# A diagonal state-space branch whose scratch transfers are issued by GpSimd instead of SyncE

## The chip, the cores and the metric

The kernel runs on one core of one Trainium2 chip. The metric is the device time of one execution in microseconds (us). Before the change it is 2403.66 us, the median of three executions that lie between 2402.31 and 2406.75 us.

## What is computed

The reference is a trunk of two layers over 272 positions (16 learned ones and 256 of the input) of width 2048, in float32. An even layer projects the normalised input to queries, keys, values and a 512 wide signal u. The first three feed grouped-query attention (12 heads, 4 key heads, rotary positions), u feeds a bidirectional diagonal complex state-space model (S5) in 32 groups of 16 channels with 64 states each; both are concatenated and projected back. An odd layer does the same with retention and an mLSTM. Each layer ends with a squared-ReLU MLP of width 8192. Only the S5 branch of the even layer matters here. Cut to its core:

```python
def s5_direction(u, lam_re, lam_im, log_dt, b_re, b_im, c_re, c_im):
    ...
    bu_re = jnp.einsum('blgh,gph->blgp', u, bbar_re)
    bu_im = jnp.einsum('blgh,gph->blgp', u, bbar_im)
    ...
    _, _, x_re, x_im = lax.associative_scan(_complex_scan_combine, (a_re, a_im, bu_re, bu_im), axis=1)
    return jnp.einsum('blgp,ghp->blgh', x_re, c_re) - jnp.einsum('blgp,ghp->blgh', x_im, c_im)
```

## The kernel before

**Weights.** Every projection is one `stream` (lines 144 to 206). It loads a stripe of the weights, 128x1024 float32 or 512 KB, into a tile `raw` (line 184, issued by SyncE; line 181 where a stripe is put together from two parts). ScalarE rounds it to `wh` (line 134), VectorE takes the rest, `wl` (line 135), and TensorE adds three products per block, wh by xh, wh by xl and wl by xh (line 168). `raw`, `wh` and `wl` have four buffers each, so a load of `raw` waits until `wl` of the stripe four before it is made.

**The even layer.** `even_in` first streams the weights of u (`w_u`, eight stripes). `first_norm` then finds the norm of the input, and for each of the four blocks of u `evac_u` scales the block into `up` (line 741) and stores it to a DRAM scratch `s5_u` (line 744). `finish_u` gathers it back as `U` with time folded by eight: eight transfers, one for each residue s, each of 16 partitions by 32 groups by 34 steps (line 751), so that its contiguous runs are 34 floats, 136 bytes. Behind that the stripes of q, k and v follow (`w_even`, 40 stripes of 512 KB) with the attention.

**The S5 branch** is a generator that is woven into that stream. It goes through eight batches of four groups. `batch` loads the coefficients `bc` (line 835, 256 KB, two buffers), scales them (line 837), builds on VectorE the tables `W` and `CA` (helper `tt`, line 754), transposes W to `WT` on TensorE (line 876), and multiplies `kps` (line 887). `CA` goes to a DRAM scratch `s5_ca` (line 890, 576 KB, one buffer for CA) for use at the end. Out of `kps` come the taps `Kf`, and eight shifted copies of `Kf` make the stripes of `M` (line 900, eight transfers of 32 KB a batch). `apply` multiplies `U` by `WT` into `pe` (line 913) and by `M` into `pm` (line 922). After the last batch the recurrence over the 34 folded steps runs on VectorE; `tail` loads `CA` again (line 979), multiplies, applies GELU and the half-GLU, and the output projection follows.

**Who sets the order.** Each engine, and each engine's issue of transfers, takes its instructions strictly in order, and an instruction that waits holds up all behind it on that engine. The order is not that of the program text. A planner makes it when the program is built, out of priorities (`high_priority` in `stream`, `batch`, `run`) and of its own model of what each instruction occupies: a transfer counts as work of the engine that issues it. SyncE (SP in the profile) issues nearly all transfers: weights, hT, u, U, bc, CA, M. GpSimd (POOL) issues four loads of constants at the start (lines 101, 545, 546, 548), and in the even layer it otherwise runs some memsets (`pt2` L578, `qr` and `sq` L598, `V` L661, the first column of EE L947); the adds of the residuals (L307) come after the layer. All of this is queued by

```python
nc.sync.dma_start(out=self.ud[ft * P:(ft + 1) * P], in_=up)
nc.sync.dma_start(out=self.U[s * 16:(s + 1) * 16], in_=v[s])
nc.sync.dma_start(out=bc, in_=I["s5_bc"][:, b])
nc.sync.dma_start(out=self.cad[b], in_=CA.rearrange("p d g t h -> p (d g t h)"))
```

Of the kernel before, what the change touches and what calls it, by code (L numbers as in the profile page):

```python
# [15 lines left out]
P = 128  # L16
# [707 lines left out]
class S5:  # L724
# [12 lines left out]
    def evac_u(self, ft):  # L737
        nc = self.nc
        acc = self.T.h[:, ft]
        up = self.p2.tile([P, S5C, S5J], F32, name="up", tag="sg")  # L740
        nc.vector.tensor_tensor(out=up.rearrange("p s j -> p j s"),
                                in0=acc.rearrange("p (j s) -> p j s", s=S5C),
                                in1=self.T.rb.rearrange("p (j s) -> p j s", s=S5C), op=ALU.mult)
        nc.sync.dma_start(out=self.ud[ft * P:(ft + 1) * P], in_=up)

    def finish_u(self):
        nc = self.nc
        self.U = self.p1.tile([P, S5G, S5J], F32, name="U")
        v = self.ud.rearrange("(g h) s j -> s h g j", h=16)
        for s in range(S5C):  # L750
            nc.sync.dma_start(out=self.U[s * 16:(s + 1) * 16], in_=v[s])

    def tt(self, out, a, b, op):
        self.nc.vector.tensor_tensor(out=out, in0=a, in1=b, op=op)
# [75 lines left out]
    def batch(self, b):  # L830
        nc, I, p1, p2, tt, T = self.nc, self.I, self.p1, self.p2, self.tt, self.T
        mul, add, sub = ALU.mult, ALU.add, ALU.subtract
        g0 = b * NB
        bc = p2.tile([P, 4, 2, NB, 16], F32, name="bc")
        nc.sync.dma_start(out=bc, in_=I["s5_bc"][:, b])
        bb = p1.tile([P, 2, 2, NB, 16], F32, name="bb")
        nc.vector.tensor_scalar_mul(out=bc[:, 2:], in0=bc[:, 2:], scalar1=self.sg[:, 1:2])
        btmp = p1.tile([P, 2, NB, 16], F32, name="btmp")

        def gsel(x):  # L840
            return x.rearrange("p (d g) -> p d g", d=2)[:, :, g0:g0 + NB].unsqueeze(3).broadcast_to([P, 2, NB, 16])

        cr, ci = gsel(self.cr), gsel(self.ci)
        tt(bb[:, 0], bc[:, 0], cr, mul)
        tt(btmp, bc[:, 1], ci, mul)
        tt(bb[:, 0], bb[:, 0], btmp, add)
        tt(bb[:, 1], bc[:, 1], cr, mul)
        tt(btmp, bc[:, 0], ci, mul)
        tt(bb[:, 1], bb[:, 1], btmp, sub)
        yield  # L850

        def table(dst, tmp, Pa, Pb, A, B, d, lo, n, rev):
            ks = slice(lo, lo + n)

            def pw(x):
                v = x[:, ks, d * S5G + g0:d * S5G + g0 + NB]
                if rev:
                    v = v[:, ::-1]
                return v.rearrange("p k g -> p g k").unsqueeze(3).broadcast_to([P, NB, n, 16])

            def cf(x):
                return x.unsqueeze(2).broadcast_to([P, NB, n, 16])

            tt(dst, pw(Pa), cf(A), mul)
            tt(tmp, pw(Pb), cf(B), mul)
            tt(dst, dst, tmp, add)

        W = p1.tile([P, 2, NB, S5C, 16], F32, name="W")
        wt = p1.tile([P, NB, 9, 16], F32, name="wtmp")
        WT = p1.tile([P, 2, NB, P], F32, name="WT")  # L870
        for d in range(2):
            table(W[:, d], wt[:, :, :S5C], self.P1, self.P2, bb[:, 0, d], bb[:, 1, d], d, 0, S5C, d == 0)
            with T.tc.high_priority(offset=URGENT):
                pt = T.mx([P, NB, P], "wtp")
                for g in range(NB):
                    nc.tensor.transpose(pt[:, g], W[:, d, g].rearrange("p s h -> p (s h)"), T.ident)
                nc.scalar.copy(out=WT[:, d], in_=pt)
            yield
        CA = p1.tile([P, 2, NB, 9, 16], F32, name="CA")
        kp = []  # L880
        for d in range(2):
            table(CA[:, d], wt, self.P1, self.P2, bc[:, 2, d], bc[:, 3, d], d, 0, 9, d == 1)
            with T.tc.high_priority(offset=URGENT):
                ps = T.mx([16, NB, P], "kps")
                for g in range(NB):
                    lo = 0 if d == 0 else 1
                    nc.tensor.matmul(ps[:, g], bb[:, 0, d, g], CA[:, d, g, lo:lo + 8], start=True, stop=True)  # L887
            kp.append(ps.rearrange("p g (t h) -> p g t h", h=16))
            yield
        nc.sync.dma_start(out=self.cad[b], in_=CA.rearrange("p d g t h -> p (d g t h)"))  # L890
        Kf = p1.tile([16, NB, 15, 16], F32, name="Kf")
        nc.scalar.copy(out=Kf[:, :, 8:15], in_=kp[0][:, :, 1:8])
        nc.scalar.copy(out=Kf[:, :, 0:8], in_=kp[1])
        tt(Kf[:, :, 7], kp[0][:, :, 0], Kf[:, :, 7], add)
        dm = p1.tile([16, NB, 16], F32, name="dm")
        tt(dm, self.drow[:, g0:g0 + NB], T.ident[:16, :16].unsqueeze(1).broadcast_to([16, NB, 16]), mul)
        tt(Kf[:, :, 7], Kf[:, :, 7], dm, add)
        M = p1.tile([P, NB, P], F32, name="M")
        for s in range(S5C):
            nc.sync.dma_start(out=M[s * 16:(s + 1) * 16].rearrange("p g (t h) -> p g t h", h=16),  # L900
                                in_=Kf[:, :, 7 - s:15 - s])
        yield
        self.batches.append((b, WT, M))
# [533 lines left out]
```

## Time and profile before

| | |
|---|---|
| median of three executions | 2403.66 us |
| the profiled execution, its own time | 2401.9 us |
| its span, first to last instruction | 2400.1 us |
| TensorE busy | 2347.3 us, 98% of the span |
| VectorE, ScalarE, GpSimd busy | 60%, 47%, 3% |
| mean granted TensorE clock | 0.991 |
| transfers | 415.52 MB, 173 GB/s over the span |

Times in the trace are us from the first instruction. The span is 1.8 us shorter than the time of its execution. A line of the waits reads: who waited, for whom, us in total, how often, the longest. In a timeline a bracket holds the idle time of the engine ahead of the instruction and what ended it. SPq and POOLq are the queues from which SyncE and GpSimd issue transfers; an issue's own duration is the time that the queue was held, and the transfer lands later.

### The profile page before, as it was taken

To read this page: it belongs to the slowest core of one execution; us is meant where nothing else is said; L and a number is where in the kernel's file an instruction comes from. 1 tells how busy PE (TensorE), PEld (TensorE's weight loads), DVE (VectorE), ACT (ScalarE), POOL (GpSimd) and SP (SyncE) were. 2 spreads that over 40 slices of the span, in tenths; PEclk is the share of its full clock that TensorE was granted. 3 is DMA by queue.
4 is the path that set the end of the run, shared out by engine and by line. 5 is a ranking of instruction groups with operands and counts; after the bars stand their busy time and mean duration, and the time that the engine had idled before them with its cause. 6 is when DMAs were issued, how large, how long until landed. Compare 5 with 4: busy or idle time off the path is not lost.

```text
span 2400.1 us, 42631 instructions
## 1 busy us (share of the span) xinstructions
PE 2347.3 (98%) x17287; PEld 2241.3 (93%) x17287; DVE 1442.0 (60%) x2365; ACT 1136.9 (47%) x1768; POOL 60.3 (3%) x116
## 2 busy tenths in 40 slices
PE   7999999999999999999989999999999999999998
PEld 7889899999999999999989999999988988988987
DVE  8786837754554454555679767656744545555555
ACT  6566735543443343344466434444544443443443
POOL 0000001100000000000110000001000000000000
PEclk9999999999999999999999999999999999999999
DMA  8545364555555555555443443564655556555554
GB/s 267 167 148 175 116 200 139 185 175 175 174 177 174 176 175 176 175 176 183 149 150 127 159 150 129 188 198 137 201 186 187 186 173 191 185 186 191 185 187 147
DMA packets 143461, 415.52 MB, mean 173 GB/s; under 512 B 24496, under 2 KB 41280, under 8 KB 142496
## 3 DMA queue, kind: packets, MB, share of 16 engines
q1 hardware_dynamic: 142816, 412.36, 53.9%
q8 instruction: 135, 2.21, 0.4%
q14 instruction: 62, 0.51, 0.1%
q0 software_dynamic: 160, 0.35, 0.1%
q10 hardware_dynamic: 288, 0.10, 0.0%
HBM read 401.62 MB, written 7.95 MB: 171 GB/s over the span
## 4 chain that ended last, share of the span: by engine, by line
PE 90%; DVE 5%; ACT 2%; issue 1%; DMA 1%; POOL 0%; SPq 0%; DVEq 0%; ACTq 0%; POOLq 0%
PE acc L168 82%; DVE wl L135 1%; ACT wh L134 1%; PE kps L887 1%; PE pe L913 1%; PE mo L1221 1%; PE po L710 1%; PE ro L1297 1%; POOL h L307 0%; PE sc L687 0%; DVE res L304 0%; DMA raw<-in_w_u 0%; PE ptp L703 0%; PE ms L1183 0%; PE rs L1288 0%
## 5 line engine op out<-in xcount | busy, mean ns | idle before, releaser
L135 DVE TENSOR_TENSOR wl<-raw,wh 128x1024 fp32r<-128x1024 f32 (+2 forms) x744 | 888.3, 1195 | 808.4 <-ACT wh L134 806.4
L134 ACT CAST wh<-raw 128x1024 fp32r<-128x1024 f32 (+2 forms) x744 | 759.9, 1023 | 1011.8 <-PE acc L168 977.1
L168 PE MATMUL acc<-xh,wh 128*128 128x272 f32 (+1 forms) x3728 | 1070.2, 288 | 18.0 <-ACT wh L134 8.7
L168 PE MATMUL acc<-xh,wl 128*128 128x272 f32 (+1 forms) x3728 | 1070.9, 288 | 11.2 <-DVE wl L135 11.1
L168 PE MATMUL acc<-xl,wh 128*128 128x272 f32 (+1 forms) x3728 | 1070.8, 288 | 3.4 <-DVE xl L135 2.3
L168 PEld LDWEIGHTS acc<-xh,wh 128*128 128x128 f32 x3728 | 706.2, 190 | 21.6 <-ACT wh L134 9.0
L168 PEld LDWEIGHTS acc<-xh,wl 128*128 128x128 f32 x3728 | 707.1, 190 | 15.9 <-DVE wl L135 14.4
L168 PEld LDWEIGHTS acc<-xl,wh 128*128 128x128 f32 x3728 | 708.7, 190 | 5.4 <-DVE xl L135 2.5
L168 PE MATMUL acc<-h1l,wh 128*128 128x272 f32 x1024 | 295.4, 288 | 0.0
L168 PE MATMUL acc<-h1h,wl 128*128 128x272 f32 x1024 | 295.2, 288 | 0.0
L168 PE MATMUL acc<-h1h,wh 128*128 128x272 f32 x1024 | 294.0, 287 | 0.0
L168 PE MATMUL acc<-wh,h1l 128*128 128x512 f32 (+1 forms) x528 | 205.1, 388 | 0.0
L168 PE MATMUL acc<-wh,h1h 128*128 128x512 f32 (+1 forms) x528 | 204.8, 388 | 0.0
L168 PE MATMUL acc<-wl,h1h 128*128 128x512 f32 (+1 forms) x528 | 203.9, 386 | 0.0
L168 PEld LDWEIGHTS acc<-h1h,wh 128*128 128x128 f32 x1024 | 192.9, 188 | 0.0
L168 PEld LDWEIGHTS acc<-h1l,wh 128*128 128x128 f32 x1024 | 192.6, 188 | 0.0
L168 PEld LDWEIGHTS acc<-h1h,wl 128*128 128x128 f32 x1024 | 192.4, 188 | 0.0
L168 PEld LDWEIGHTS acc<-wh,h1l 128*128 128x128 f32 x528 | 99.1, 188 | 22.0
L168 PEld LDWEIGHTS acc<-wl,h1h 128*128 128x128 f32 x528 | 99.3, 188 | 21.7
L168 PEld LDWEIGHTS acc<-wh,h1h 128*128 128x128 f32 x528 | 99.4, 188 | 21.1
L307 POOL TENSOR_TENSOR h<-h,res 128x272 f32<-128x272 f32 (+1 forms) x42 | 43.8, 1053 | 568.0 <-DVE res L304 568.0
L382 ACT ACTIVATE relu<-acc 128x272 f32<-128x272 f32 (+1 forms) x128 | 48.7, 387 | 17.6 <-PE acc L168 17.6
(319 smaller groups left out, 1506.5 us busy)
## 6 DMA issues: line engine op xcount, KB each, us to landing
raw<-in_w SPq DMA_DIRECT2D x480, 512.0 KB, 3.5
raw<-in_w_odd SPq DMA_DIRECT2D x88, 512.0 KB, 3.4
raw<-in_w_even SPq DMA_DIRECT2D x40, 512.0 KB, 4.4
raw<-in_wo_odd SPq DMA_DIRECT2D x24, 512.0 KB, 3.6
raw<-in_wo_a SPq DMA_DIRECT2D x24, 384.0 KB, 4.3
raw<-in_w SPq DMA_DIRECT2D x32, 256.0 KB, 2.6
s_ca<-CA SPq DMA_DIRECT2D x8, 576.0 KB, 3.3
CA<-s_ca SPq DMA_DIRECT2D x8, 576.0 KB, 4.3
```

The source lines that it names most:

```text
L134: nc.scalar.copy(out=hi, in_=src)
L135: nc.vector.tensor_tensor(out=lo, in0=src, in1=hi.bitcast(F32), op=ALU.subtract)
L168: nc.tensor.matmul(a, lt, rt, start=k == 0 and j == 0, stop=k == nk - 1 and j == 2)
L307: eng.tensor_tensor(out=self.h[:, k, t0:], in0=self.h[:, k, t0:], in1=t[:, :N], op=ALU.add)
L382: nc.scalar.activation(out=t[:, :N], in_=acc, func=AF.Relu)
L710: nc.tensor.matmul(po[:, :R // 2], cur["v", g][:, j], PT[j][:, c0:c0 + R // 2], start=j == 0, stop=j == 2)
L887: nc.tensor.matmul(ps[:, g], bb[:, 0, d, g], CA[:, d, g, lo:lo + 8], start=True, stop=True)
L913: nc.tensor.matmul(pev[:, d, g], WT[:, d, g], U[:, g0 + g], start=True, stop=True)
L1221: nc.tensor.matmul(po[:, d, :HD + 1], e[:, t:t + P], V[:, st], start=j == 0, stop=j == len(keys) - 1)
L1297: nc.tensor.matmul(po[:, :HD], w[:, j, t:t + P], self.rvt[:, h, j], start=j == 0, stop=j == 2)
```

## The change

The four stores of `up`, the eight gathers of `U`, the eight loads of `bc` and the eight stores of `CA` (28 transfers) are issued by GpSimd. The 64 stripes of `M`, all weights, and all of the tail stay on SyncE.

```diff
@@ evac_u @@
-        nc.sync.dma_start(out=self.ud[ft * P:(ft + 1) * P], in_=up)
+        nc.gpsimd.dma_start(out=self.ud[ft * P:(ft + 1) * P], in_=up)
@@ finish_u @@
-            nc.sync.dma_start(out=self.U[s * 16:(s + 1) * 16], in_=v[s])
+            nc.gpsimd.dma_start(out=self.U[s * 16:(s + 1) * 16], in_=v[s])
@@ batch @@
-        nc.sync.dma_start(out=bc, in_=I["s5_bc"][:, b])
+        nc.gpsimd.dma_start(out=bc, in_=I["s5_bc"][:, b])
@@ batch @@
-        nc.sync.dma_start(out=self.cad[b], in_=CA.rearrange("p d g t h -> p (d g t h)"))
+        nc.gpsimd.dma_start(out=self.cad[b], in_=CA.rearrange("p d g t h -> p (d g t h)"))
```

## Rows read from the trace of the kernel before

**Rows 1.** The page: busy time, share of the span and instructions by engine.

```profile
PE 2347.3 (98%) x17287; PEld 2241.3 (93%) x17287; DVE 1442.0 (60%) x2365; ACT 1136.9 (47%) x1768; POOL 60.3 (3%) x116
```

**Rows 2.** Busy time by stretch: us, engines (instructions), granted clock, DMA share, GB/s.

```profile
54.90:73.00 18.10, 15.51 (x112) 15.29 (x112) 11.83 (x19) 3.87 (x7) 0.00 (x0) 0.91 0.67 127
73.00:126.00 53.00, 51.79 (x406) 47.31 (x406) 40.80 (x94) 33.54 (x67) 0.17 (x1) 1.00 0.52 171
126.00:202.00 76.00, 75.43 (x552) 67.11 (x552) 56.33 (x126) 53.82 (x111) 0.71 (x4) 1.00 0.47 149
202.00:232.00 30.00, 30.00 (x241) 28.66 (x240) 21.34 (x34) 15.56 (x28) 0.21 (x1) 1.00 0.60 171
```

**Rows 3.** Waits of SyncE's queue over the whole span.

```profile
SPq L900 <- DVE Kf L754: 27.1, 8, 6.2
...
SPq L890 <- DVE CA L754: 14.2, 6, 7.9
...
SPq L835 <- DVE dm L754: 6.0, 1, 6.0
```

**Rows 4.** SyncE's queue in order of time, 41 to 70 us (equal neighbours are merged).

```profile
41.70 6.27 SPq L900 DMA_DIRECT2D M<-Kf  x8
48.07 1.01 SPq L744 DMA_DIRECT2D s_u<-up  x2
...
49.62 0.45 SPq L184 DMA_DIRECT2D raw<-in_w_even  x1
51.40 0.86 SPq L744 DMA_DIRECT2D s_u<-up  x2
52.35 0.89 SPq L184 DMA_DIRECT2D raw<-in_w_even  x2
54.91 6.41 SPq L751 DMA_DIRECT2D U<-s_u  x8
69.27 0.34 SPq L890 DMA_DIRECT2D s_ca<-CA  x1
69.73 0.35 SPq L184 DMA_DIRECT2D raw<-in_w_even  x1
```

**Rows 5.** Waits of TensorE from 40 to 70 us, then from 70 to 100 us.

```profile
PE acc L168 <- DVE wl L135: 2.6, 1, 2.6
...
PE acc L168 <- DVE wl L135: 0.6, 1, 0.6
```

**Rows 6.** ScalarE, then VectorE, in order of time, 44 to 76 us.

```profile
53.98 1.05 ACT L134 CAST wh<-raw 128x1024 fp32r<-128x1024 f32 x1 [7.39 <-DMA raw<-in_w_even]
58.06 0.40 ACT L624 ACTIVATE sqt<-acc 128x272 f32<-128x272 f32 x1 [3.03 <-PE acc L168]
...
59.85 2.00 ACT L134 CAST wh<-raw 128x1024 fp32r<-128x1024 f32 x2
...
75.71 0.35 DVE L837 TENSOR_SCALAR bc<-bc,sgn 128x256 f32<-128x256 f32 x1 [6.46 <-DMA bc<-in_s_bc]
```

**Rows 7.** Moved issues (ns min/median/max, first, last start); one issue of GpSimd (timeline).

```profile
L751 SPq DMA_DIRECT2D U<-s_u x8: 340/488/2629, 54.9 to 60.7; - x8
...
L835 SPq DMA_DIRECT2D bc<-in_s_bc x8: 328/435/897, 5.1 to 159.5; - x8
...
L890 SPq DMA_DIRECT2D s_ca<-CA x8: 326/326/338, 36.6 to 213.6; - x8
...
1.94 0.54 POOL L545 DMA_DIRECT2D cosE<-in_rope_even  x1
```

**Rows 8.** Who needs U first, and median us from issue to landing.

```profile
L913 PEld LDWEIGHTS pe<-U,WT x128: 186/192/192, 72.6 to 221.6; 128*128 128x128 f32 x128
...
s_u<-up SPq DMA_DIRECT2D x4, 136.0 KB, 2.9
U<-s_u SPq DMA_DIRECT2D x8, 68.0 KB, 5.7
...
cosE<-in_rope_even POOLq DMA_DIRECT2D x1, 136.0 KB, 5.7
```

## The prediction

> **What bounds the kernel now.** The first view is the page's busy time: TensorE is busy for 98% of the span and GpSimd for 3% [rows 1]. A change of issuing queues can therefore win only what TensorE loses in the stage where the moved transfers run, so the second view is the stretches of that stage. In the last of them, 202 to 232 us, TensorE runs 241 instructions in 30 us, 8.03 per us [rows 2]; I take this as its full rate. At that rate the 18.1 us from 54.9 would hold 145 instructions and hold 112: 33 are missing, 4.1 us. From 73 to 126 us 426 would fit and 406 are there: 2.5 us. From 126 to 202 us 610 would fit and 552 are there: 7.2 us [rows 2]. There the attention's softmax runs, with VectorE and ScalarE busy for 56 and 54 of 76 us.
>
> The third view is what SyncE's queue waits for. It waits 14.2 us ahead of the stores of CA and 6.0 us once ahead of a load of bc; all that time the weights queued behind are not issued. It also waits 27.1 us ahead of the stripes of M [rows 3], and those stay. The timeline of that queue shows the place: after the first eight stripes of M it issues two stores of u, a load of raw, two stores more, two loads of raw, then eight gathers of U in 6.41 us, and it stands until 69.27 us at a store of CA with the next raw behind it [rows 4]. The fourth view asks whether late weights are what TensorE waits for. Its recorded waits there are 2.6 us for wl in the first 30 us, and 0.6 us for wl later [rows 5]. ScalarE has waited 7.39 us for raw before the cast at 53.98 us, but the next cast, at 59.85 us, stands behind evacuations that start at 58.06 us, once TensorE's accumulation is over [rows 6]: late weights make themselves felt here through the order of ScalarE's queue.
>
> **The change part by part.**
>
> *SyncE's queue.* It loses 28 issues: four of u in 1.87 us [rows 4], eight of U by 0.488, eight of bc by 0.435 and eight of CA by 0.326 us [rows 7], together 1.9 + 3.9 + 3.5 + 2.6 = 11.9 us of issuing, and the 14.2 us and 6.0 us of waits. By itself that is worth nothing: the engine computes nothing, and TensorE covers it with stripes already loaded.
>
> *The weights behind it.* The three loads of raw at 49.62, 52.35 and 52.8 us could leave from 47.97 us on, where the stripes of M end [rows 4], as their buffers come free: up to 1.6, 4.4 and 4.8 us earlier. The raw at 69.73 us could leave up to 7 us sooner, for no issue is left ahead of it. How much reaches TensorE depends on the order in which the planner then puts casts and evacuations. If the order on the other engines stays, nothing does: TensorE has enough to do up to 58 us, and the evacuations still stand ahead of the second cast. If the earlier stripe lets the cast go ahead of them, the wait of 2.6 us is gone. The ends are 0 and the 6.6 us that the two stretches lose (4.1 + 2.5). I take the waits that the profile records, 2.6 + 0.6 = 3.2 us: ScalarE sits idle before the first cast for longer than a cast takes, and the planner charges a transfer to the engine that issues it, so in its model too the weights get earlier.
>
> *bc.* VectorE idles 6.46 us at 75.71 us for bc [rows 6], whose load was queued behind the gathers and a store of CA. It has two buffers, so on GpSimd's queue it can leave when its buffer is free, if nothing there waits ahead of it. Gain: nothing beyond the 3.2 us, since TensorE is busy while VectorE idles.
>
> *u and U.* The last store of u is issued at about 51.9 us, lands 2.9 us later [rows 8], and the first gather follows at 54.91 us [rows 4]: it waits for a landing, not for SyncE. Here GpSimd can lose. One of its issues held its queue for 0.54 us [rows 7], but that transfer had 128 runs and a gather has 16 x 32 = 512. The lower bound is 0.34 us, the shortest on SyncE; the upper 4 x 0.54 = 2.2 us, runs in proportion. I take 1.0 us, nearer to 0.54, the only price of this queue: eight gathers are out by 62.9 us and, with 5.7 us to land [rows 8], U is there at 68.6 us. TensorE first reads it at 72.6 us [rows 8]. Cost 0, with 4 us to spare; the point from which it costs is 1.5 us a gather (54.9 + 8 x 1.5 + 5.7 = 72.6).
>
> *CA.* A store leaves when the table is ready, as now (the one at 69.27 us stood at the head of its queue). The next batch's table needs the single buffer back; the eight stores lie between 36.6 and 213.6 us [rows 7], 25 us apart in the mean, which covers a landing even at the 5.7 us of GpSimd's transfer [rows 8]. Cost 0.
>
> *GpSimd's queue.* 28 issues by 0.54 us are 15.1 us, or by the upper bound for U 28 us, on an engine that runs five instructions between 73 and 202 us [rows 2]. They are memsets of the attention, and some wait for TensorE; a bc behind one, or a memset behind a store of CA, inherits its wait. VectorE waits for bc, ScalarE's copy of V for the memset. I cost this at nothing: the waits of one engine's order are exchanged for those of another with far fewer members.
>
> *Sum.* 2401.9 us, the profiled execution (span 2400.1 and 1.8 around it), less 3.2 is 2398.7. That execution lies 1.8 us under the median, 2403.7, so against the median the forecast is 2403.7 - 3.2 = **2400.5 us**, 0.13% less. About 0.2% of it, 4.8 us, is what a measurement of this kernel can tell from no change.
>
> **The rivals.**
>
> *A, hidden anyway.* The stripes of M stay with their 27.1 us of waits, so weights are still queued behind waiting transfers, and no cast moves ahead of an evacuation. For it: only 3.2 us of TensorE's waits are recorded at all. Against it: the one idle stretch of ScalarE is ended by raw itself. Time 2403.7 us. The Trainium skill, page "DMA: Bandwidth & Descriptors", section "Issuing engines are not separate DMA queues", gives this result by a rule: transfers run on the same 16 engines whoever issues them, and several issuers save only the time of issuing, usually small. By that rule the time stays 2403.7 us; the trace agrees as far as the issues alone go (11.9 us, off the path), but the queue's in-order waits, 14.2 us for CA alone, are moved too.
>
> *B, the whole loss comes back.* With weights, bc and tables earlier, TensorE runs at full rate from 54.9 to 126 us: 6.6 us, 2397.1 us. For it: half of the queue's waits go, and VectorE's idle 6.46 us lies right before the stretch where it is busiest. Against it: the evacuations and the tables stay in order. If the better order also fills the attention's stretch, 7.2 us more, 2389.9 us.
>
> *C, U comes late.* GpSimd makes the 512 runs of each gather at the upper price: the last is out at 54.9 + 8 x 2.2 = 72.5 us, landed at 78.2 us, and pe, which was to start at 72.6 us, holds TensorE's queue for 5.6 us with all products behind it. Time 2409.3 us, slower. For it: the only priced transfer of that queue has a quarter of the runs. Against it: the planner can put other products ahead of pe. It decides the sign above 1.5 us a gather and passes 0.2% above 2.1 us. If the stores of u also land in 5.7 instead of 2.9 us, 2.8 us more, 2412.1 us.
>
> **How the numbers follow.** The forecast has 0.36, with a range of its own of 2398 to 2403: its terms may come out between half and one and a half, and of its chance 0.08 lies beyond 4.8 us of gain. A has 0.13, B 0.28, C 0.23, of which 0.01 stays within 4.8 us. So faster 0.28 + 0.08 = 0.36, within 0.2% 0.28 + 0.13 + 0.01 = 0.42, slower 0.22. The range is 2390 to 2411 us: from B with its attention stretch to C short of its late stores. It leaves out some 0.1 on each side, where the planner's new order moves work that no row here ties to the moved transfers.
>
> **What would show it.** Right: SyncE's queue shows raw right behind the first eight stripes of M; its waits ahead of CA and bc are gone and those of M still there; TensorE's wait of 2.6 us near 58 us is gone; from 54.9 to 126 us some 25 instructions more; the gathers of U on GpSimd's queue 1 us apart, landed before pe. Wrong: TensorE waiting for U at pe; a cast still behind the evacuations, with the same rates (A); or a difference that arises after 232 us, where none of the moved transfers runs, which would mean that the planner's order, not the queue's waits, sets the result.

## The result, and the profile after

The changed kernel takes 2417.35 us, the median of four executions between 2415.65 and 2418.65 us; the kernel before, run beside it, takes 2403.02 us. The ratio on record is 1.0051, with a 95% interval from 1.0039 to 1.0063: 0.51% or some 12 us slower, where 0.13% faster was forecast. (It is not the quotient of the two medians, which is 1.0060 and lies inside the interval.) The two executions that were profiled lie further apart than the medians, 14.3 us: their spans are 2416.8 and 2400.1 us, so what follows accounts for 16.7 us.

The page of the changed kernel, its first part, answers to [rows 1].

```profile
PE 2354.2 (97%) x17287; PEld 2244.7 (93%) x17287; DVE 1443.4 (60%) x2365; ACT 1137.2 (47%) x1768; POOL 76.0 (3%) x144
```

GpSimd has 28 instructions more, the transfers. TensorE does the same work and is busy for 6.9 us more (its mean granted clock is 0.987 against 0.991), so of the 16.7 us at least 9.8 are spent standing. Where, is read from the stretches. First the changed kernel:

```profile
28.00:41.70 13.70, 10.87 (x81) 9.34 (x80) 13.70 (x22) 9.95 (x12) 1.08 (x2) 1.00 0.82 298
41.70:54.90 13.20, 12.86 (x94) 12.33 (x93) 10.36 (x26) 7.30 (x12) 1.30 (x3) 0.93 0.71 231
54.90:73.00 18.10, 18.10 (x139) 17.92 (x139) 15.29 (x24) 5.96 (x8) 7.20 (x12) 0.96 0.72 152
73.00:126.00 53.00, 53.00 (x429) 50.90 (x429) 39.45 (x70) 29.07 (x49) 1.62 (x3) 1.00 0.57 187
126.00:202.00 76.00, 75.25 (x568) 68.36 (x567) 55.38 (x130) 49.32 (x101) 3.94 (x10) 1.00 0.44 145
202.00:232.00 30.00, 27.39 (x177) 22.84 (x175) 20.19 (x41) 19.86 (x45) 0.90 (x3) 0.94 0.17 49
232.00:299.00 67.00, 63.38 (x436) 55.75 (x437) 47.46 (x172) 48.56 (x109) 0.16 (x1) 0.95 0.50 161
299.00:347.00 48.00, 47.63 (x349) 45.40 (x348) 23.59 (x68) 17.22 (x30) 0.00 (x0) 0.93 0.56 170
347.00:400.00 53.00, 47.94 (x334) 45.48 (x334) 28.43 (x46) 21.71 (x37) 0.00 (x0) 0.94 0.60 176
```

Then the stretches of the kernel before that do not stand in [rows 2]:

```profile
28.00:41.70 13.70, 12.33 (x92) 11.03 (x93) 13.70 (x26) 9.53 (x12) 0.00 (x0) 1.00 0.77 266
41.70:54.90 13.20, 13.20 (x103) 12.72 (x103) 9.09 (x23) 5.29 (x9) 0.21 (x1) 1.00 0.54 166
232.00:299.00 67.00, 64.13 (x434) 56.89 (x433) 56.98 (x214) 49.22 (x110) 0.17 (x1) 0.97 0.45 142
299.00:347.00 48.00, 47.79 (x342) 46.34 (x342) 15.21 (x27) 15.82 (x26) 0.00 (x0) 0.93 0.70 204
347.00:400.00 53.00, 52.17 (x418) 51.95 (x416) 34.65 (x56) 26.44 (x43) 0.00 (x0) 1.00 0.55 169
```

Count TensorE's instructions against before. From 28 to 54.9 us there are 20 fewer (175 against 195). From 54.9 to 202 us, where the forecast expected a gain, there are 66 more (1136 against 1070): that gain came, and larger than forecast. Then 64 fewer from 202 to 232 us, 9 more up to 347 us, and 84 fewer from 347 to 400 us. The balance from 28 us on is 93 fewer at 400 us, which at 8.03 per us is 11.6 us. The gain is early, the loss late.

The chain of waits of both kernels, up to 440 us, says what is late. Before:

```profile
72.93 1.71 PE pe L913 x16
...
335.00 4.25 DMA gT<-s_y
339.38 7.57 PE glu L1005 x32
346.95 49.86 PE acc L168 x399
402.43 0.85 PE pb L243 x6
```

After:

```profile
52.49 36.88 PE acc L168 x279
89.37 1.71 PE pe L913 x16
...
355.09 4.00 DMA gT<-s_y
359.22 9.75 PE glu L1005 x32
368.97 43.88 PE acc L168 x351
...
416.18 1.48 PE pb L243 x6
```

The changed kernel's wait of TensorE for a cast, between 300 and 370 us, which the kernel before does not have:

```profile
PE acc L168 <- ACT wh L134: 4.1, 1, 4.1
```

The first product of U into pe is at 89.4 instead of 72.9 us, 16.4 us later. In the chain the next batches' pe follow at 98.5, 113.6 and 129.8 us where before they stood at 83.1, 97.7 and 115.1: some 15 us late, and the last at 238.4 against 220.2, 18 us late. The half-GLU behind the tail starts 19.8 us late. Behind it TensorE has 351 products of the stream left instead of 399, since 48 more are done already; at 49.86/399 = 0.125 us each that gives 6.0 us back. The GLU itself takes 9.75 instead of 7.57 us, 2.2 us more: TensorE has run out of cast weights ahead of it, waits 4.1 us until 357.2 us, and the granted clock during the GLU is 0.77, before 1.00. From the last of these products to pb it takes 2.3 us less. So pb, the broadcast of the norm with which the even layer's output is closed, comes 19.8 + 2.2 - 6.0 - 2.3 = 13.7 us later (416.18 - 402.43 = 13.75). From there to the end the two take about the same, 2000.6 and 1997.7 us; these 2.9 us are the rest of the 16.7.

And pe is not held up by U. TensorE's recorded waits from 55 to 75 us are gone altogether, and no wait of pe for U is among those up to 130 us. What stands ahead of pe is other work, 52.49 to 89.37 us without a gap in the chain. One of the three products of a block, counted up to the first pe, first before, then after:

```profile
L168 PE MATMUL acc<-xh,wh x120: 283/288/592, 8.5 to 72.4; 128*128 128x272 f32 x120
```

```profile
L168 PE MATMUL acc<-xh,wh x164: 282/288/596, 7.1 to 88.8; 128*128 128x272 f32 x164
```

Three products each: 360 of the stream ahead of the first pe before, 492 after. The planner has put 132 products more in front of it.

The moved transfers themselves, in the timelines of SyncE's and of GpSimd's queue after, answer to [rows 4]:

```profile
42.88 5.73 SPq L900 DMA_DIRECT2D M<-Kf  x8
48.71 42.95 SPq L184 DMA_DIRECT2D raw<-in_w_even  x16
...
50.99 0.55 POOL L744 DMA_DIRECT2D s_u<-up  x1 [11.40 <-DVE up L741]
59.39 0.54 POOL L744 DMA_DIRECT2D s_u<-up  x1 [0.37 <-DVE up L741]
62.03 5.00 POOL L751 DMA_DIRECT2D U<-s_u  x8 [2.10 <-DMA s_u<-up]
```

The groups by tile (issues and landings) and the wait of SyncE for M, after, answer to [rows 3, 7, 8]:

```profile
L751 POOL DMA_DIRECT2D U<-s_u x8: 628/628/652, 62.0 to 66.4; - x8
DMA to landing us min/median/max: 6.2/8.4/9.0
...
L835 POOL DMA_DIRECT2D bc<-in_s_bc x8: 536/538/561, 4.3 to 174.4; - x8
...
L890 POOL DMA_DIRECT2D s_ca<-CA x8: 531/542/570, 39.1 to 230.5; - x8
...
SPq L900 <- DVE Kf L754: 44.7, 6, 24.5
```

raw follows the first eight stripes of M at once, SyncE's waits for CA and bc are gone, a gather holds GpSimd's queue for 0.628 us. But u is scaled later (up from 50.1 to 58.4 us; before 46.9 to 51.2), the gathers leave at 62.0 instead of 54.9 us and land in 8.4 instead of 5.7 us, and SyncE once waits 24.5 us ahead of a stripe of M, with weights behind it: the transfers of 202 to 232 us fall from 171 to 49 GB/s.

### The profile page after: what moved, and what is told of

Its sections match the earlier page's. It is cut to its first block, busy times and chain, and to the rows that moved or that the text cites. A ratio compares the mean times of both kernels' runs of the same rounds, so it can differ in the third digit from the quotient of the medians.

```text
span 2416.8 us, 42664 instructions
## 1 busy us (share of the span) xinstructions
PE 2354.2 (97%) x17287; PEld 2244.7 (93%) x17287; DVE 1443.4 (60%) x2365; ACT 1137.2 (47%) x1768; POOL 76.0 (3%) x144
## 4 chain that ended last, share of the span: by engine, by line
PE 87%; DVE 5%; ACT 3%; DMA 2%; issue 1%; POOL 1%; SPq 0%; DVEq 0%; ACTq 0%; POOLq 0%
PE acc L168 79%; DVE wl L135 2%; ACT wh L134 1%; DVE res L304 1%; POOL h L307 1%; PE pe L913 1%; PE kps L887 1%; PE mo L1221 1%; ACT pe L692 1%; PE po L710 0%; PE ro L1297 0%; DVE z L754 0%; PE glu L1005 0%; PE pc L233 0%; DVE xl L138 0%
## 5 line engine op out<-in xcount | busy, mean ns | idle before, releaser
L168 PEld LDWEIGHTS acc<-xh,wh 128*128 128x128 f32 x3728 | 706.5, 190 | 26.5 <-ACT wh L134 12.0
```

The lines of the kernel that those rows point to most:

```text
L168: nc.tensor.matmul(a, lt, rt, start=k == 0 and j == 0, stop=k == nk - 1 and j == 2)
```

## The experiments

Three theories. **P**, the planner's order: with U's gathers on GpSimd it puts some 130 products ahead of the first pe, and the S5 chain, which is serial to the GLU, is late by that. **Q**, the price of the transfers: on GpSimd they leave and land later, and the chain is late by that. **S**, SyncE's queue: its wait of 24.5 us ahead of M starves TensorE of weights from 202 us on.

All ratios are against the kernel before on the same chip; its median is 2403.02 us for the row "after" and lies between 2406.5 and 2407.9 us for e1 to e12. "Ahead" is the number of products of the stream ahead of the first pe, in the order of TensorE's queue; the starts of the first pe (of its weight load, up to 0.3 us ahead of the product in the chains of waits) and of the GLU are those of the profiled execution. The row "before" comes from the first chip, where this kernel is 3 to 5 us faster than on the others, so small differences between starts of different rows carry nothing.

| run | ahead | first pe, us | GLU, us | median, us | ratio (95%) |
|---|---|---|---|---|---|
| before | 360 | 72.6 | 339.4 | | |
| after | 492 | 89.1 | 359.2 | 2417.35 | 1.0051 (1.0039 to 1.0063) |
| e1, only U's gathers moved | 489 | 91.5 | 358.3 | 2417.09 | 1.0034 (1.0023 to 1.0046) |
| e2, all moved but U's gathers | 384 | 75.7 | 344.6 | 2410.90 | 1.0012 (1.0002 to 1.0022) |
| e3, after with pe early | 384 | 77.3 | 355.1 | 2412.69 | 1.0028 (1.0015 to 1.0042) |
| e4, before with pe late | 490 | 95.1 | 360.6 | 2417.82 | 1.0044 (1.0028 to 1.0061) |
| e5, after with pe at 360 | 360 | 76.1 | 345.6 | 2409.72 | 1.0012 (1.0003 to 1.0021) |
| e6, before with pe at 312 | 312 | 66.3 | 338.6 | 2408.98 | 1.0009 (0.9999 to 1.0019) |
| e7, as e5, bc on SyncE | 360 | 71.7 | 343.3 | 2407.86 | 1.0005 (0.9996 to 1.0014) |
| e8, only bc moved | 384 | 75.3 | 341.6 | 2404.32 | 0.9990 (0.9981 to 0.9999) |
| e9, before with pe at 425 | 425 | 87.5 | 353.0 | 2418.66 | 1.0041 (1.0025 to 1.0058) |
| e10, as e8, pe at 360 | 360 | 72.6 | 343.4 | 2408.25 | 1.0003 (0.9994 to 1.0013) |
| e11, as e8 again | 384 | 76.4 | 343.4 | 2405.43 | 0.9988 (0.9978 to 0.9998) |
| e12, U's gathers by ScalarE | 313 | 72.9 | 346.2 | 2410.60 | 1.0012 (1.0002 to 1.0022) |

Two readings go through all fourteen profiled executions. From pb to the end they take 1997.7 to 2001.8 us, while pb itself starts between 402.4 and 418.1 us: what sets them apart has nearly all happened by the end of the even layer. And TensorE waits once for a cast shortly ahead of the GLU in the changed kernel (4.1 us), e1 (5.5), e4 (5.7) and e9 (4.8), the four with the highest ratios; in none of the others does it wait more than 0.3 us for a cast between 300 and 370 us.

### Which of the transfers: e1 and e2

e1 moves the gathers alone, e2 the other twenty alone. The edit of e1, then that of e2:

```diff
-            nc.sync.dma_start(out=self.U[s * 16:(s + 1) * 16], in_=v[s])
+            nc.gpsimd.dma_start(out=self.U[s * 16:(s + 1) * 16], in_=v[s])
```

```diff
-        nc.sync.dma_start(out=self.ud[ft * P:(ft + 1) * P], in_=up)
+        nc.gpsimd.dma_start(out=self.ud[ft * P:(ft + 1) * P], in_=up)
-        nc.sync.dma_start(out=bc, in_=I["s5_bc"][:, b])
+        nc.gpsimd.dma_start(out=bc, in_=I["s5_bc"][:, b])
-        nc.sync.dma_start(out=self.cad[b], in_=CA.rearrange("p d g t h -> p (d g t h)"))
+        nc.gpsimd.dma_start(out=self.cad[b], in_=CA.rearrange("p d g t h -> p (d g t h)"))
```

> Only the eight gathers of U go to GpSimd; u, bc and CA stay on SyncE. Theory P (the planner's order): the gathers alone make the planner put the first pe behind 489 products of the stream on TensorE's queue instead of 360, the serial S5 chain starts some 16 us later and the end of the even layer with it: 2413 to 2419 us, pe first near 88 us. Theory Q (the price of GpSimd's transfers: U lands in 8.4 instead of 5.7 us, CA in 6.4 instead of 3.3 us): only U's 2.7 us are left, 2403 to 2407 us. Theory S (SyncE stands 24.5 us ahead of stripes of M because bc and CA wait for each other on GpSimd's queue): bc and CA are back, so 2402 to 2405 us.

> u's stores, bc and CA go to GpSimd; the gathers of U stay on SyncE. Theory P: the first pe stands behind 384 products and the tail's first py behind 1302 (before: 360 and 1305), so no loss: 2399 to 2406 us. Theory Q: CA and bc keep their slower landings: 2408 to 2417 us. Theory S: the wait of some 24 us ahead of M stays: 2412 to 2417 us.

e1 brings most of the loss with it, 1.0034, and pe stands at 91.5 us; e2 leaves 1.0012 with pe at 75.7 us. The ranges of the expectations of e1 to e4 go by a kernel before of some 2403 us, while on this chip it takes 2407.9 us, so they are read as differences: e1 loses 8.2 us, where P asked 10 to 16 and Q 0 to 4, and e2 loses 2.9 us, at the upper end of P's -4 to +3. So the gathers' issuer decides the greater part. That alone does not tell P from Q, for the gathers are also the transfers that pe needs. Of e1, the gathers and their landing:

```profile
L751 POOL DMA_DIRECT2D U<-s_u x8: 628/631/652, 55.7 to 60.0; - x8
DMA to landing us min/median/max: 8.1/10.3/11.7
```

They leave from 55.7 us on, earlier than in the changed kernel, and are issued by 60.0 + 0.6 us; with the longest landing, 11.7 us, the last is there at 72.3 us. pe follows at 91.5 us, behind 489 products: it does not wait for them. S falls here too: SyncE's waits ahead of M are 26.5 us in eight, the longest 7.8 us; before they are 27.1 us, the longest 6.2 us [rows 3].

### The order by itself: e3 and e4

Both add an edge that fixes an order on TensorE's queue and adds no wait of its own. e3 takes the changed kernel and puts the 385th product of the stream behind the sixteen first products of pe. e4 takes the kernel before, where no transfer is moved, and puts those behind the 490th product. The edge, as in e4 (e3 swaps the two ends and has `FIRST = 384`; the lines that collect the first products of pe into `pe0` are left out here):

```diff
+FIRST = 489
...
-                nc.tensor.matmul(a, lt, rt, start=k == 0 and j == 0, stop=k == nk - 1 and j == 2)
+                mm = nc.tensor.matmul(a, lt, rt, start=k == 0 and j == 0, stop=k == nk - 1 and j == 2)
+                self.count(mm)
...
+    def count(self, mm):
+        self.nmm += 1
+        if self.pe0 is not None and self.nmm > FIRST:
+            for i in self.pe0:
+                self.tc.add_manual_dep(i.ins, mm.ins.name, mybir.DependencyInfo(mybir.DependencyClass.NoSync, mybir.DependencyReason.DATA))
+            self.pe0 = None
```

> The changed kernel (all 28 transfers on GpSimd) with one edge of order without a wait: the 385th product of the stream is queued behind the first pe. TensorE's order is then close to that of before (pe behind 384, first py behind 1301, GLU behind 1502 products, before 360, 1305 and 1502). Theory P: the loss is gone, 2400 to 2407 us; TensorE may stand a few us at pe, since U lands near 75 us. Theory Q: the transfers are as slow as in the changed kernel, 2413 to 2419 us. Theory S: 2412 to 2419 us.

> The kernel before (all transfers on SyncE) with one edge of order without a wait: the first pe is queued behind the 490th product, as far back as in the changed kernel (492). No transfer is moved. Theory P: it loses what the change loses, 2413 to 2419 us. Theory Q and S: no transfer of GpSimd's, so 2402 to 2406 us.

e4 is the run that decides. With every transfer where it was, the order alone costs 0.44%, which the interval does not separate from the 0.51% of the change. Its products ahead of pe, its wait ahead of M, TensorE's wait between 300 and 370 us, the end of its chain and the last stretch:

```profile
L169 PE MATMUL acc<-xh,wh x163: 282/288/594, 7.7 to 94.7; 128*128 128x272 f32 x163
...
SPq L912 <- DVE Kf L766: 26.6, 8, 7.8
...
PE acc L169 <- ACT wh L135: 5.7, 1, 5.7
...
360.55 9.62 PE glu L1022 x32
370.17 39.37 PE acc L169 x315
415.09 0.85 PE pb L255 x6
...
347.00:400.00 53.00, 46.64 (x326) 44.21 (x326) 27.33 (x45) 21.94 (x37) 0.00 (x0) 0.94 0.74 172
```

pe behind 490 products (the first line ends just ahead of the last of them), GLU at 360.6 us, pb at 415.1 us and 326 instructions in the last stretch: the changed kernel's picture (492, 359.2, 416.2 and 334), without its wait of 24.5 us. The loss does not need that wait, so S is refuted as its main cause. e4 is no exact copy, though. The edge names one place, and the planner laid out the rest anew; TensorE also waits 4.9 us for a cast ahead of pe and runs at a granted clock of 0.50 (the lower level, 1.2 GHz) from 76.2 to 81.4 us behind it, so pe is at 95.1 us, 6 us later than in the changed kernel.

e3 recovers only part, 1.0028 or 6.7 us, between P's -3 to +4 and Q's 10 to 16, and its GLU is at 355.1 us although pe is at 77.3. It has the widest scatter of all, 2410.7 to 2423.0 us; the profiled execution is one of the long ones, with a granted clock of 0.89 to 0.90 from 42 to 126 us. It also fixes one product alone and leaves the later batches to the planner. A stricter form follows.

### The order of before, with the transfers moved: e5 and e6

e5 takes the changed kernel, with all 28 transfers on GpSimd, and puts each of the products 361 to 553 behind the last of the first pe. e6 does the same to the kernel before from product 313 on, so that pe comes 48 products sooner than in any kernel so far. The edge, in place of the one above:

```diff
+FIRST = 360
...
+        if self.pe0 is not None and self.nmm > FIRST:
+            self.tc.add_manual_dep(mm.ins, self.pe0[-1].ins.name,
+                                    mybir.DependencyInfo(mybir.DependencyClass.NoSync, mybir.DependencyReason.DATA))
+            if self.nmm > FIRST + 192:
+                self.pe0 = None
```

> All 28 transfers on GpSimd, and every product from the 361st on is queued behind the first pe, so TensorE's order is that of before (pe behind 360, 370, 448, 524, 612, 697, 864 and 955 products; before 360, 370, 438, 532, 611, 696, 864 and 955). Theory P alone: as fast as before, within 3 us. P with a price for the late start of u (bc's two early loads share the start's bandwidth, U is gathered 7 us later and lands 3 us slower): TensorE stands some 3 to 6 us at the first pe, 3 to 7 us over the kernel before. Theory Q: 10 us or more over it.

> The kernel before with no transfer moved; every product from the 313th on is queued behind the first pe, which moves up 48 products, some 6 us of TensorE. If the S5 chain from the first pe to the end of the branch is what bounds the even layer (theory P), the first pe comes 4 to 6 us earlier and the run gains 2 to 5 us on the kernel before. If TensorE's total work bounds it (as the prediction had it), no change within 1 us, or a loss where TensorE stands at pe for U (landed near 67 us).

e5 measures 1.0012: three quarters of the loss go when the order alone is put back. For the rest, some 3 us, there is a candidate. Of e5, the gathers, their landing, TensorE's wait and the end of the chain:

```profile
L764 POOL DMA_DIRECT2D U<-s_u x8: 628/630/652, 62.4 to 66.8; - x8
DMA to landing us min/median/max: 6.9/8.8/9.8
...
PE pe L927 <- DMA U<-s_u: 2.9, 1, 2.9
...
345.61 7.57 PE glu L1023 x32
353.19 49.87 PE acc L169 x399
408.62 1.48 PE pb L256 x6
```

Now pe does wait for U, 2.9 us, and starts at 76.1 instead of 72.6 us. That would be Q, at a quarter of its stated weight, hidden by the order of the changed kernel; it is not shown, for e7 below waits 2.4 us at the same place and loses nothing that can be told. Behind the GLU there are 399 products again, in the same 49.87 us.

e6 is against the strong form of P, in which every product taken out from ahead of pe is worth its time. pe starts 6.3 us sooner than before, after a wait of 2.6 us for U, the GLU 0.8 us sooner, and the time is 1.0009, no gain where P asked 2 to 5 us. Late costs; early did not pay here.

### What is left: e7, e8, e10 and e11

e7 is e5 with bc's loads back on SyncE; e8 moves bc alone, and e11 is e8 again on another chip; e10 is e8 with the edge of e5. The edit of e8 (e7 leaves out this one):

```diff
-        nc.sync.dma_start(out=bc, in_=I["s5_bc"][:, b])
+        nc.gpsimd.dma_start(out=bc, in_=I["s5_bc"][:, b])
```

> u, U and CA on GpSimd, bc on SyncE, TensorE's order as before (as in the run that moves all 28). If bc's early loads are what delays u: u is scaled near 47 us as before, U lands by 70 us, the time is within 2 us of before. If U's and CA's landings on GpSimd cost: 3 to 7 us over before.

> Only the eight loads of bc go to GpSimd; the planner puts the first pe behind 384 products (before 360), the rest close to before. If bc's early loads delay the start and u: 2 to 5 us over before, with the first gather of U near 61 us instead of 54.9. If bc costs nothing: within 2 us of before, or a gain of 1 to 3 us from VectorE's wait of 6.46 us for bc.

> Only bc on GpSimd, and the products from the 361st on queued behind the first pe (without the edge it stands behind 384). If bc's gain is VectorE's wait for bc and the 24 products cost nothing: 1 to 4 us under before, like bc alone. If TensorE stands at pe for U, which is gathered 5 us later with bc's early loads: within 2 us of before.

> The same as the run with bc alone, again: ratio 0.998 to 1.0 if its small gain is real, around 1.001 if it was the chip's scatter.

e7 measures 1.0005, no difference that can be told. Its up is at 46.6 to 54.8 us where e5 has 50.1 to 58.8 and e8 50.1 to 57.1, so it is bc's issuer that shifts the start of the scaling of u. The cost of 2 to 5 us that could follow from that did not come: e8 is at 0.9990 and e11 at 0.9988, both intervals below 1, though only just. Moving bc alone is worth some 0.1%, 2 to 3 us, and is the one version that beats both kernels. That is the size expected from VectorE's wait for bc, but hardly that mechanism: this wait is still 6.1 us in e8 and 6.8 us in e11, against 7.2 us before. With the order held at 360 (e10) the time is 1.0003; its interval and those of e8 and e11 overlap, so whether the gain comes with those 24 products more ahead of pe is not settled.

### How the price grows, and another issuer: e9 and e12

e9 is e4 with `FIRST = 424`, half the way. e12 lets ScalarE issue U's gathers, and nothing else is changed:

```diff
-            nc.sync.dma_start(out=self.U[s * 16:(s + 1) * 16], in_=v[s])
+            nc.scalar.dma_start(out=self.U[s * 16:(s + 1) * 16], in_=v[s])
```

> The kernel before, no transfer moved, with the first pe queued behind the 425th product (before behind 360, in the run with the same edge at 490 behind 490: 10 us over before). In the kernel before, TensorE still has 63 products of the stream to do after the branch's GLU that do not need it, some 7.7 us of slack. If delay beyond that slack is what costs: the branch ends some 8 us later, and the run is 0 to 4 us over before. If every us of delay costs: half of 130 products, 5 us over before or more.

> Only the gathers of U move, to ScalarE's queue instead of GpSimd's; the planner then puts the first pe behind 313 products, not 489. Theory P (the place of pe, not the leaving of SyncE): no loss of the size that the gathers on GpSimd have, within 4 us of before, with TensorE standing a few us at pe for U and ScalarE's casts held by eight issues. If leaving SyncE's queue as such costs: 8 us or more over before.

Half the products cost nearly the whole: 1.0041 against e4's 1.0044. pe is at 87.5 us, 14.9 us later than before, while 65 products at the full rate are 8.1 us. Neither a slack of some products nor a straight line through e4 fits. TensorE's waits for casts in e9, from 40 to 110 us and from 300 to 370 us, and the stretch behind the first of them:

```profile
PE acc L169 <- ACT wh L135: 3.2, 1, 3.2
...
PE acc L169 <- ACT wh L135: 4.8, 1, 4.8
...
76.28:80.50 4.22, 4.13 (x16) 3.81 (x17) 3.02 (x4) 2.28 (x3) 0.00 (x0) 0.50 1.02 398
```

The edge fixes the place of pe only, and the planner laid out the rest anew. So part of the lateness is not the products ahead: TensorE runs out of cast weights, waits 3.2 us, and has a granted clock of 0.50 behind that, its lower level (1.2 GHz). The second wait, ahead of the GLU, is the one that e4 has too.

e12 has 313 products ahead of pe, one more than e6, and TensorE waits 1.8 us for U and 6.9 us for a cast of ScalarE, which now issues the gathers too; its GLU is at 346.2 us and it measures 1.0012. So it is not the leaving of SyncE as such that pushes pe back: by ScalarE pe moves forward, by GpSimd back.

## Why the prediction was wrong

*What bounds.* "A change of issuing queues can therefore win only what TensorE loses in the stage where the moved transfers run": this is the sentence that failed. It takes the time to be TensorE's throughput, stage by stage. The time is also the length of a serial chain, from pe to the recurrence, the tail and the GLU, behind which 399 products and the layer's norm stand. The changed kernel has 66 instructions more in the stages the forecast looked at (50 of them up to 126 us, where some 25 were expected) and loses, because products done early are missing later, while the chain is on its way: 64 fewer from 202 to 232 us, 84 fewer from 347 to 400 us, where TensorE waits 4.1 us for a cast ahead of the GLU.

*SyncE's queue and the weights behind it.* Right in all that can be seen: raw directly behind the first eight stripes of M, the waits ahead of CA and bc gone, TensorE's 2.6 us near 58 us gone. The 3.2 us were not kept, because those products went ahead of pe. The 11.9 us of issuing take a gather at its median; in [rows 4] the eight hold the queue for 6.41 us, which makes it 14.4 us, worth nothing either way.

*u and U.* "Cost 0, with 4 us to spare" was the step on which it turned. The sum let pe stay at 72.6 us, and asked only whether U would be there; measured, pe is at 89.1 us, 16.5 us later, behind 132 more products, with U there by 76 us. The price of a gather, 1.0 us taken between 0.34 and 2.2, measured 0.628 us; four times the runs of the constants' load took 1.16 times its 0.54 us, not four times. But the gathers left 7.1 us later, since up was later, and landed 2.7 us later in the median. With pe at its old place TensorE waits 2.9 us for them (e5). What cost the greater part was that pe did not stay there.

*bc, CA, GpSimd's queue.* bc alone gains 0.1% (e8, e11) where nothing beyond the 3.2 us was expected; VectorE's wait for bc did not go with SyncE's: it is 9.4 us in the changed kernel, 7.2 us before. CA was moved alone in no run; together with others it stands in e2 and e7, which lose 0.12% and 0.05%, at most 0.22% and 0.14% by their intervals. No run ties a loss to the order of GpSimd's own queue, and none tried it alone.

*The rivals.* C had the sign, for another reason: its 2.2 us a gather and its 5.6 us of TensorE standing at pe did not come, and its "the planner can put other products ahead of pe", meant as a relief, is the loss itself. B's rate came, 568 instructions from 54.9 to 126 us where the full rate gives 571, and its time did not. A's time is that of a kernel in which the transfers are hidden; with the order of before, e7 comes to it and e5 within 3 us. The Trainium skill's page "DMA: Bandwidth & Descriptors", section "Issuing engines are not separate DMA queues", says that starting transfers from several engines saves only the time of starting them, which is usually small. Once the order is held, the runs agree to 0.12% (e10 1.0003, e7 1.0005, e5 1.0012, its interval just above 1); the greater part of the 0.51% comes from the planned order, of which the section does not speak.

*The sum.* Half to one and a half of 3.2 us is 2398.9 to 2402.1 us, so the forecast's own range, 2398 to 2403 us, was a little wider than its reason, and the 0.08 beyond 4.8 us of gain had none. This did not decide anything.

*What would make it wrong.* The last of the signs named was "a difference that arises after 232 us, where none of the moved transfers runs, which would mean that the planner's order, not the queue's waits, sets the result". The order is what sets the result (e4, e5), but only 84 of the 148 instructions that are missing late are missing after 232 us; the other 64 are from 202 to 232 us, where moved transfers still run. It should have been a rival with a price: the planner's freedom to shift pe among the products around it could have been bounded by the time from pe to the GLU and the products left behind the GLU, both in the chain of waits of before.

**What stays open.** Why the planner puts pe 132 products later when GpSimd issues the gathers, and earlier when ScalarE does, was seen in the order and not traced into its model. Why 65 products cost about as much as 130 is not settled: both e9 and e4 have the wait ahead of the GLU, but what it costs was not tried by itself. Nor is it settled why e3, which does not have it, recovered less than e5. The profiled executions of one kernel differ by up to 5 us (e8 and e11), so differences of a few us among GLU starts carry nothing.

## What to carry to other kernels

Where a planner orders the engines, moving a transfer to another issuer moves compute instructions too: count what stands ahead of the transfer's first reader before and after, and follow the start of the serial chain, not the busy share of the engine it feeds. To tell the order from the transfer, hold the order with an edge that adds no wait of its own, once in the changed kernel and once reversed in the kernel before. And look at what the edge itself brings: here it left TensorE short of cast weights for some us. An engine busier in one stage gains nothing if that work was the filler for a later wait.

## What the runs showed of the hardware

In the changed kernel GpSimd's queue was held for 0.53 to 0.57 us by each of the 20 moved transfers of 128 rows, and for 0.63 to 0.65 us by a gather of 512 runs of 136 bytes: four times the runs, a sixth more time. The gathers also landed later: their median is 7.4 to 10.3 us in the five runs in which GpSimd issued them, 3.7 to 6.4 us in the eight in which SyncE did; whether that is the issuer or the loads of raw that leave beside them is not told apart. For bc there is no such difference (medians of 3.1 to 5.8 us in seven runs against 2.8 to 5.6 us in seven). In e12 a gather held ScalarE's queue for 0.328 us, the median, and those landed in 6.5 us. TensorE's granted clock was 0.50 from 76.3 to 80.5 us in e9 and from 76.2 to 81.4 us in e4, right behind waits of 3.2 and 4.9 us.
